# Shift chunks of a modulated input projection moved from TensorE to VectorE, with three edits of banks and loads

## The chip, the cores and the metric

The kernel runs on one core of a Trainium2 chip. The metric is the device time of one execution in microseconds (us). A core has TensorE (PE, matmuls, results in PSUM banks of 128x512 fp32), VectorE (DVE), ScalarE (ACT), GpSimd (POOL) and SyncE (SP, which here only issues loads). Each engine works through its own queue of instructions in order, and waits on semaphores for the others.

## The reference

One layer, in fp32: 512 latent tokens `x` and 256 context tokens `ctx`, width 2048.

```python
mx = silu(c) @ w_mod + b_mod            # and mc from c_ctx, for the context
sh1, sc1, gt1, sh2, sc2, gt2 = split(mx, 6)
hc = rmsnorm(ctx, norm1_g) * (1 + sc1c) + sh1c
hx = rmsnorm(x, norm1_g) * (1 + sc1) + sh1
q, k, v, g, lf, lb, cb, cc, cx = split_proj(hx @ w_in)   # k 512, v 1024 columns; lf, lb 16 each
la_f = log_sigmoid(lf @ w_gf + b_gf) / 16                # la_b likewise
o = gated_linear_attention(q, k, v, la_f, la_b, state_of_context)   # both directions
mix = concat([rmsnorm(o) * gla_g * silu(g), cb * conv3(cc * cx)]) @ w_out
x1 = x + gt1 * mix
h2 = rmsnorm(x1, norm2_g) * (1 + sc2) + sh2
out = rmsnorm(x1 + gt2 * (silu(h2 @ w_ffn_gate) * (h2 @ w_ffn_up)) @ w_ffn_down, final_g)
```

The shift `sh1` (2048 numbers for x, 2048 for the context) is a product of silu(c) with 2048 columns of `w_mod`.

## The kernel before

The inner dimension 2048 is cut into 16 chunks of 128 (`KD`). Tokens stand in six tiles of 128: four of x, two of the context. fp32 operands are split into two parts, hi and lo (`hhi`/`hlo`, for odd chunks side by side in `hhl`, for the context in `chl`), and `mm3` makes a product from three matmuls. Weights arrive as `raw` (128x1024, two K tiles, four buffers), ScalarE casts them to `whi`, and VectorE subtracts for `wlo` (L107).

The stages that matter here:

- K. `scaled_chunk` builds each chunk scaled, but not normalised and not shifted, and K is computed from it. The missing rsqrt (`r6` by token, `rbx` and `rbc` as broadcast rows) is applied to the results.
- First half of V (`wv[0]`), 16 K tiles of 18 matmuls. Alongside, `mod_cols(wsh, ...)` computes four groups of four chunks of the shift on TensorE: 16 blocks of 32 columns into the bank `pm`, a copy, then `pc`, which stands the result up as columns `shs`. From tile 4 on `shift_chunk(i - 4)` makes the chunk final: GpSimd adds hi and lo, VectorE multiplies by the rsqrt row and adds the shift, both split again. `lf_part` computes the low-rank rows (`pl`) from the shifted chunks.
- Second half of V (`wv[1]`), from shifted chunks. Alongside, `shares` adds what the shift contributes to the results that were computed without it: it loads the weights once more and multiplies them by `shs` (`pb`, then `pbc`, `pbk`, `pbx`).
- Context gates and q; then `do_gates`, with `log_gates` (a chain of two Abs, Exp, Ln on ScalarE and two instructions on VectorE, L497) for each token tile; GLA heads, output projection, FFN. During all this `mod_some` computes the other modulation numbers on VectorE: rows of `wm2` multiplied by a broadcast row `cbc` of silu(c) and summed (L405).
- The FFN's down projection works on block combinations: operand pairs `a0h` to `a6l` are loaded from DRAM (`load_ops`), weight parts `ch` as well (`back`), and steps "1", "7", "63", "5" stand in a fixed order. The last group adds by rows (`by_rows`); its last tile is done in two column halves, which share one bank.

Banks come from rings: `bank` has five, `abank` three. The order on each engine is not that of the code: a scheduler sets it when the program is built, from due times of its own, so that a load or a product may stand far from its line.

## Time and profile before

| | |
|---|---|
| median of 3 runs | 2288.15 us (2282.64 to 2289.99) |
| profiled execution | 2291.32 us, span 2289.5 us |
| mean granted clock of TensorE | 0.993 |
| busy: PE, DVE, ACT, POOL | 2241.7, 1658.7, 1002.6, 251.0 us |
| DMA | 433 MB, 189 GB/s over the span |

In the rows of a profile a line starts with the start and the length in us, then come engine, line, operation, outputs<-inputs by the names of the program, and the shape. What stands in brackets is the engine's idle time before and what ended it. `PE acc L94 <- DVE wlo L107: 12.6, 12, 3.2` in a list of waits means 12.6 us in 12 waits, the longest 3.2. Lines of a group give the count, the busy time and the mean in ns.

### The profile page before, as it was taken

The numbers are of one execution on the slowest core, as the hardware profiler recorded it, in microseconds if no ns is written. First come the engines' busy times: TensorE is split into PE (matmuls) and PEld (weight loads), VectorE is DVE, ScalarE is ACT, GpSimd is POOL, SyncE is SP. The second block draws the span as 40 slices with busy tenths as digits, with TensorE's granted clock in tenths as the row PEclk, the third lists the DMA queues.
The fourth block names the chain that finished last, engine by engine and source line by source line (L and its number), as shares of the span: only waits on it lengthen the run. The fifth ranks groups of instructions, "written<-read, shape, count | busy, mean of one in ns | idle before, by whom it ended". The sixth has DMA issues, their size and how long they took to land.

```text
span 2289.5 us, 28001 instructions
## 1 busy us (share of the span) xinstructions
PE 2241.7 (98%) x10258; PEld 1791.7 (78%) x10258; DVE 1658.7 (72%) x2069; ACT 1002.6 (44%) x1354; POOL 251.0 (11%) x396
## 2 busy tenths in 40 slices
PE   8999999999999999999999999999999999999997
PEld 4765666787888887777888888888888878888886
DVE  3566165665768656899788879877987877787885
ACT  3433155333233433665555455445544544433343
POOL 2433100222332000100000000000000000000000
PEclk9999999999999999999999999999999999999999
DMA  9683465566767354624543464345435676756752
GB/s 329 216 279 129 153 221 189 202 220 202 250 228 258 116 198 157 208 69 141 189 156 120 147 210 148 118 159 172 158 131 183 246 291 212 244 193 206 253 174 93
DMA packets 163410, 433.16 MB, mean 189 GB/s; under 512 B 18022, under 2 KB 38790, under 8 KB 163144
## 3 DMA queue, kind: packets, MB, share of 16 engines
q1 hardware_dynamic: 128984, 331.20, 43.3%
q0 software_dynamic: 22416, 78.66, 9.7%
q10 hardware_dynamic: 11872, 21.52, 2.5%
q8 instruction: 81, 1.33, 0.2%
q14 instruction: 57, 0.47, 0.1%
HBM read 380.95 MB, written 50.35 MB: 188 GB/s over the span
## 4 chain that ended last, share of the span: by engine, by line
issue 56%; POOL 2%; PE 1%; DVE 1%; ACT 0%; DMA 0%; POOLq 0%; DVEq 0%; ACTq 0%
POOL opd L1066 2%; PE acc L94 1%; DVE wlo L107 0%; DVE ch L849 0%; DMA out<-g 0%; DVE u L1019 0%; POOL xnd L1022 0%; ACT whi L106 0%; POOL hbig L958 0%; DVE hbig L1020 0%; DVE u L869 0%; POOLq L1066 0%; ACT y L1214 0%; ACT acc L1205 0%; DVE g L1202 0%
## 5 line engine op out<-in xcount | busy, mean ns | idle before, releaser
L106 ACT CAST whi<-ch 128x1024 fp32r<-128x1024 f32 x335 | 352.5, 1053 | 415.4 <-PE acc L94 344.9
L107 DVE TENSOR_TENSOR wlo<-ch,whi 128x1024 fp32r<-128x1024 f32 x335 | 408.2, 1223 | 126.9 <-ACT whi L106 126.0
L106 ACT CAST whi<-raw 128x1024 fp32r<-128x1024 f32 x258 | 270.7, 1050 | 453.6 <-PE acc L94 282.0
L107 DVE TENSOR_TENSOR wlo<-raw,whi 128x1024 fp32r<-128x1024 f32 x258 | 316.6, 1227 | 198.3 <-ACT whi L106 197.7
L94 PE MATMUL acc<-hhl,whi 128*128 128x512 f32 x640 | 200.0, 393 | 0.0
L94 PEld LDWEIGHTS acc<-hhl,whi 128*128 128x128 f32 x640 | 120.8, 189 | 27.6 <-issue 2.5
L1066 POOL DMA_DIRECT2D opd<-ol x80 | 43.3, 541 | 885.8 <-DVE ol L107 885.7
L94 PE MATMUL acc<-hhi,wlo 128*128 128x512 f32 x320 | 134.1, 421 | 5.4 <-DVE wlo L107 4.6
L405 DVE CUSTOM_DVE_ANT_0 wm<-wm,cbc 128x1024 f32<-128x1024 f32 x66 | 80.6, 1224 | 80.9 <-DMA wm<-wm 80.2
L94 PE MATMUL acc<-wlo,a0h 128*128 128x512 f32 x324 | 128.8, 397 | 4.0 <-DVE wlo L107 4.0
L94 PE MATMUL acc<-whi,a6l 128*128 128x512 f32 (+1 forms) x330 | 127.9, 389 | 2.4 <-ACT acc L1205 2.1
L94 PE MATMUL acc<-wlo,a6h 128*128 128x512 f32 (+1 forms) x330 | 128.1, 388 | 1.3 <-DVE wlo L107 1.3
L94 PE MATMUL acc<-whi,a6h 128*128 128x512 f32 (+1 forms) x330 | 127.8, 387 | 0.0
L94 PE MATMUL acc<-whi,a0h 128*128 128x512 f32 x324 | 127.5, 393 | 0.0
L94 PE MATMUL acc<-hlo,whi 128*128 128x512 f32 x320 | 126.9, 397 | 0.2 <-DVE hlo L112 0.2
L94 PE MATMUL acc<-hhl,wlo 128*128 128x512 f32 x320 | 127.0, 397 | 0.0
L94 PE MATMUL acc<-whi,a0l 128*128 128x512 f32 x324 | 126.9, 393 | 0.0
L94 PE MATMUL acc<-whi,a5h 128*128 128x512 f32 x324 | 126.3, 390 | 0.0
L94 PE MATMUL acc<-hhi,whi 128*128 128x512 f32 x320 | 126.2, 394 | 0.0
L94 PE MATMUL acc<-whi,a5l 128*128 128x512 f32 x324 | 126.2, 389 | 0.0
L94 PE MATMUL acc<-wlo,a5h 128*128 128x512 f32 x324 | 126.1, 389 | 0.0
L405 DVE CUSTOM_DVE_ANT_0 raw<-raw,cbc 128x1024 f32<-128x1024 f32 x62 | 75.4, 1223 | 51.4 <-DMA raw<-wm 51.1
(334 smaller groups left out, 4991.8 us busy)
## 6 DMA issues: line engine op xcount, KB each, us to landing
raw<-wu SPq DMA_DIRECT2D x92, 512.0 KB, 4.4
ch<-wu SPq DMA_DIRECT2D x88, 512.0 KB, 3.8
wm<-wm POOLq DMA_DIRECT2D x66, 512.0 KB, 5.3
raw<-wd SPq DMA_DIRECT2D x50, 512.0 KB, 5.3
raw<-wc SPq DMA_DIRECT2D x48, 512.0 KB, 4.7
opd<-oh ACTq DMA_DIRECT2D x80, 256.0 KB, 3.2
opd<-ol POOLq DMA_DIRECT2D x80, 256.0 KB, 3.7
ch<-wd SPq DMA_DIRECT2D x38, 512.0 KB, 4.4
```

What stands on the lines that cost most here:

```text
L94: nc.tensor.matmul(o, l, r, start=start, stop=stop, skip_group_check=True)
L106: nc.scalar.copy(hi, src)
L107: (eng or nc.vector).tensor_tensor(lo, src, hi, op=ALU.subtract)
L405: nc.vector.tensor_tensor_reduce(out=w, in0=w, in1=cbc[:, hf * 1024 : hf * 1024 + 1024], scale=1.0, scalar=0.0, op0=ALU.mult, op1=ALU.add, ...
L1066: nc.gpsimd.dma_start(opd[j][i, 1].rearrange("p k t -> p (k t)"), lo.bitcast(F32))
```

## The change

1. Only the first four chunks of the shift (`NPE`) stay with `mod_cols` on TensorE. For the other twelve `shift_rows` has GpSimd load transposed rows of `w_mod` (`wst`) in halves of 128x1024 and VectorE multiply and sum them: once with `cbc` (for x, 1024 elements) and twice with a part of `ccbc` (for the context, 512 elements each). 20 of the 24 halves stand in the loop of the first half of V, four in the second.
2. The second half of V and the low-rank rows are computed from rows without shift, like K and the first half. `lf_part` adds hi and lo on GpSimd for x and the context; `lf_shift` adds the shift's part later; `shares` gets eight more weight loads and `shared(2)`. The context chunks are never shifted, and the x chunks only in the second half.
3. In `do_gates` the second `pzs` of a pair comes from `abank`. In the first down group the operand loads of S2 and S4 and the weight part of the step "5" change places. In the last group the second column half of the last tile has a bank of its own, and its matmuls are cut in two from the start.

```diff
+NPE = 4
...
     def shift_chunk(i):
-        for n, h, rb, q in ((SEQ, hx[i], rbx, 0), (CTX, hc[i], rbc, 1)):
-            t = big() if q == 0 else hcpool.tile([P, n], F32, tag="sq1", name="ht", bufs=2)
-            nc.gpsimd.tensor_tensor(t, h[0].bitcast(F32), h[1].bitcast(F32), op=ALU.add)
-            nc.vector.tensor_tensor(t, t, rb, op=ALU.mult)
-            sh = shs[:, i, q : q + 1]
-            if q == 0:
-                nc.vector.tensor_scalar(t, t, sh, None, op0=ALU.add)
-                split(h[0], h[1], t)
-                hraw[i] = t
-            else:
-                split_shifted(h[0], h[1], t, sh)
+        h, t = hx[i], big()
+        nc.gpsimd.tensor_tensor(t, h[0].bitcast(F32), h[1].bitcast(F32), op=ALU.add)
+        nc.vector.tensor_tensor(t, t, rbx, op=ALU.mult)
+        split_shifted(h[0], h[1], t, shs[:, i, 0:1])
...
-    def lf_part(pl, g):
-        for j in range(4):
-            mm(pl[32 * j : 32 * j + 32, :], wl3[:, 4 * g + j, :], hraw[4 * g + j], g == 0, g == 3)
-    def lf_finish(pl, a, n):
+    def lf_part(plx, plc, g):
+        tx, tcx = [big() for _ in range(4)], []
+        for c in range(4):
+            i = 4 * g + c
+            if c % 2 == 0:
+                t2 = hcpool.tile([P, 2, CTX], F32, tag="sq0", name="hs", bufs=2)
+            tcx.append(t2[:, c % 2, :])
+            for t, h in ((tx[c], hx[i]), (tcx[c], hc[i])):
+                nc.gpsimd.tensor_tensor(t, h[0].bitcast(F32), h[1].bitcast(F32), op=ALU.add)
+        for pl, t, n in ((plx, tx, SEQ), (plc, tcx, CTX)):
+            for c in range(4):
+                mm(pl[32 * c : 32 * c + 32, :n], wl3[:, 4 * g + c, :], t[c], g == 0, g == 3)
+    def lf_finish(pl, a, n, rb):
         t = hcpool.tile([P, SEQ], F32, tag="lfs", name="lfs", bufs=1)
-        nc.scalar.copy(t[:, :n], pl[:, :n])
+        nc.vector.tensor_tensor(t[:, :n], pl[:, :n], rb, op=ALU.mult)
         ps = bank("ps")
         for q in (0, 64):
             mm(ps[q : q + 32, :n], smt[:, S_QUAD : S_QUAD + 32], t[:, :n], True, True)
         nc.scalar.copy(lfT[:32, a : a + n], ps[:32, :n])
         nc.vector.tensor_copy(lfT[64:96, a : a + n], ps[64:96, :n])
+    def lf_shift():
+        plb, t, b = bank("plb"), modv[:, 16:18], modv[:, 20:22]
+        for k in range(KD):
+            j = 32 * (k % 4)
+            mm(plb[j : j + 32, 0:2], wl3[:, k, :], shs[:, k, 0:2], k < 4, k >= 12)
+        nc.scalar.copy(t, plb[:, 0:2])
+        ps = bank("ps")
+        for q in (0, 64):
+            mm(ps[q : q + 32, 0:2], smt[:, S_QUAD : S_QUAD + 32], t, True, True)
+        for q in (0, 64):
+            nc.vector.tensor_copy(b[q : q + 32], ps[q : q + 32, 0:2])
+            for n, (c0, c1) in enumerate(((0, SEQ), (SEQ, SEQ + CTX))):
+                v = lfT[q : q + 32, c0:c1]
+                nc.vector.tensor_scalar(v, v, b[q : q + 32, n : n + 1], None, op0=ALU.add)
...
+    nc.sync.dma_start(cbc, crow.partition_broadcast(P))
+    nc.scalar.activation(cbc, cbc, AF.Silu)
+    ccbc = [big() for _ in range(4)]
+    for q in range(4):
+        nc.sync.dma_start(ccbc[q], ccrow[q * 512 : q * 512 + 512].partition_broadcast(P))
+        nc.scalar.activation(ccbc[q], ccbc[q], AF.Silu)
+    waste = big()
+    nst = KD - NPE
+    accx = modacc[:, :nst, :]
+    accc = modacc[:, nst : 3 * nst, :].rearrange("p (n q) h -> p n (q h)", q=2)
+    done = [0]
+    def shift_rows(halves, w0):
+        for _ in range(halves):
+            n, hf = divmod(done[0], 2)
+            done[0] += 1
+            w = wpool.tile([P, 1024], F32, tag="raw", name="raw", bufs=4)
+            nc.gpsimd.tensor_copy(w[:, 0:1], w0[0][:, 0, 0:1].bitcast(F32))
+            nc.gpsimd.dma_start(w, wst[n, :, hf * 1024 : hf * 1024 + 1024])
+            for q in (2 * hf, 2 * hf + 1):
+                nc.vector.tensor_tensor_reduce(
+                    out=waste, in0=w[:, q % 2 * 512 : q % 2 * 512 + 512], in1=ccbc[q], scale=1.0, scalar=0.0,
+                    op0=ALU.mult, op1=ALU.add, accum_out=accc[:, n, q : q + 1])
+            nc.vector.tensor_tensor_reduce(
+                out=w, in0=w, in1=cbc[:, hf * 1024 : hf * 1024 + 1024], scale=1.0, scalar=0.0,
+                op0=ALU.mult, op1=ALU.add, accum_out=accx[:, n, hf : hf + 1])
+            if done[0] % 8 == 0:
+                n0 = n - 3
+                for q, acc in enumerate((accx, accc)):
+                    t = modv[:, 4 * q : 4 * q + 4]
+                    nc.vector.tensor_reduce(t, acc[:, n0 : n0 + 4, :], axis=mybir.AxisListType.X, op=ALU.add)
+                    k = NPE + n0
+                    nc.vector.tensor_tensor(shs[:, k : k + 4, q], t, colt[:, C_BMOD + k : C_BMOD + k + 4], op=ALU.add)
     accv = banks6()
-    pl = bank("pl")
     for i in range(KD):
         if i % 2 == 0:
             wvp = load_w(wv[0, i // 2], 2)
         for tt in range(NX + NCT):
             mm3(accv[tt], stat(i, tt), sl(wvp, ALL, i % 2), i == 0, i == KD - 1)
-        if i % 4 == 3:
-            pcs = mod_cols(wsh, i - 3, 4)
-            for c in range(4):
-                nc.vector.tensor_scalar(shs[:, i - 3 + c, 0:2], pcs[:, 2 * c : 2 * c + 2], col(C_BMOD + i - 3 + c),
+        if i == 1:
+            pcs = mod_cols(wsh, 0, NPE)
+            for c in range(NPE):
+                nc.vector.tensor_scalar(shs[:, c, 0:2], pcs[:, 2 * c : 2 * c + 2], col(C_BMOD + c),
                                         None, op0=ALU.add)
-        if i >= 4:
-            shift_chunk(i - 4)
-        if i in (8, 12):
-            lf_part(pl, i // 4 - 2)
+        shift_rows(2 if i % 4 == 1 else 1, wvp)
+        if i in (4, 7, 10, 13):
+            if i == 4:
+                plx, plc = bank("plx"), bank("plc")
+            lf_part(plx, plc, i // 3 - 1)
+    lf_finish(plx, 0, SEQ, rbx)
+    lf_finish(plc, SEQ, CTX, rbc)
...
-    nc.sync.dma_start(cbc, crow.partition_broadcast(P))
-    nc.scalar.activation(cbc, cbc, AF.Silu)
...
-        w = load_raw((wk if i < 8 else wv[0])[i % 8]).rearrange("p (k n) -> p k n", k=2)
+        w = load_raw((wk, wv[0], wv[1])[i // 8][i % 8]).rearrange("p (k n) -> p k n", k=2)
...
+        if i % 8 == 7 and i < 16:
+            shared(i // 8)
...
-        if i < 4:
-            shift_chunk(KD - 4 + i)
-        if i == 1:
-            lf_part(pl, 2)
-        elif i == 5:
-            lf_part(pl, 3)
-            lf_finish(pl, 0, SEQ)
-        if i > 5:
-            for k in ((2 * i - 12, 2 * i - 11) if i < 12 else (i,)):
-                shares(k)
-    for tt in range(NX):
-        for hh in range(2):
-            if tt % 2 == 0:
-                vx[2 + hh][tt // 2] = xpool.tile([P, 2, DV], F32, tag="t", name="vx")
-            nc.scalar.copy(vx[2 + hh][tt // 2][:, tt % 2, :], accv[tt][:, hh * DV : hh * DV + DV])
-    for tt in range(NCT):
-        vc[tt][1] = big()
-        nc.vector.tensor_copy(vc[tt][1], accv[NX + tt])
-    lf_finish(sh_t["pl"], SEQ, CTX)
+        if i < 2:
+            shift_rows(2, wvp)
+        else:
+            for k in (0, 1) if i == 2 else (i - 1,):
+                shift_chunk(k)
+        if i == 3:
+            lf_shift()
+        if i > 3:
+            shares(2 * i - 8)
+            shares(2 * i - 7)
+    from_banks(1)
+    shift_chunk(KD - 1)
+    shared(2)
...
-            pzs = [bank("pzs") for _ in range(2)]
+            pzs = [bank("pzs"), abank("pzs")]
...
+            parts = [(tt, bank8("acc"), 0, NB) for tt in range(NX)]
+            if by_rows and c:
+                h = NB // 2
+                parts[3:] = [(3, parts[3][1], 0, h), (3, bank8("acc"), h, NB)]
...
-            def before_5():
-                if p == 0 and g == 0:
-                    load_ops(g, S2, S4)
-                    back(NPU - 1)
-
-            before = {"5": before_5, "63": before_63}
+            before = {"63": before_63}
+            if p == 0 and g == 0:
+                before["5"] = lambda: back(NPU - 1)
+                before["5", 2] = lambda: load_ops(g, S2)
+                before["5", 3] = lambda: load_ops(g, S4)
...
-        "wsh": w_mod[:, 0:2048].reshape(KD, P, D),
+        "wsh": w_mod[:, : NPE * P].reshape(KD, P, -1),
+        "wst": w_mod[:, NPE * P : 2048].T.reshape(KD - NPE, P, D),
```

Three places show what the built order makes of it. The first is GpSimd in the first half of V; `raw` with a number is one load's buffer, `wst` the new rows. Before, after the casts of the mask:

```order
L273 CAST maskt_83<-cstt_80 128x128 x8
L307 TENSOR_TENSOR big_1299<-hhi_144,hlo_145 128x512
L307 TENSOR_TENSOR big_1328<-hhl_188 128x512
L307 TENSOR_TENSOR big_1363<-hhi_264,hlo_265 128x512
L307 TENSOR_TENSOR ht_1369<-chl_271 128x256
L424 TENSOR_TENSOR hs_2085<-chl_149 128x256
L307 TENSOR_TENSOR ht_1458<-chl_311 128x256
```

After (rows 53 to 60, before these, are eight more adds of the same kind):

```order
L325 TENSOR_TENSOR big_1573<-hhi_615,hlo_616 128x512
L325 TENSOR_TENSOR big_1574<-hhl_656 128x512
L325 TENSOR_TENSOR big_1575<-hhi_732,hlo_733 128x512
L325 TENSOR_TENSOR big_1576<-hhl_773 128x512
L325 TENSOR_TENSOR big_1683<-hhi_849,hlo_850 128x512
L384 COPY raw_1343<-whi_1321 128x1
L384 COPY raw_1391<-whi_1321 128x1
L384 COPY raw_1397<-whi_1321 128x1
L325 TENSOR_TENSOR big_1684<-hhl_890 128x512
L385 DMA raw_1343<-wst 128x1024
```

The adds of thirteen x chunks now stand ahead of the load of the sixth half row (`raw_1343`); before there were three, and no load at all.

The second is VectorE at the same time, around the weight split of K tiles 6 and 7. Before, with `wlo_1342` for these tiles:

```order
L371 TENSOR_TENSOR big_1069<-big_1069,big_1096 128x512
L371 TENSOR_TENSOR big_1071<-big_1071,big_1096 128x512
L371 TENSOR_TENSOR big_1073<-big_1073,big_1096 128x512
L107 TENSOR_TENSOR wlo_1342<-raw_1339,whi_1341 128x1024
L107 TENSOR_TENSOR wlo_1466<-raw_1463,whi_1465 128x1024
L308 TENSOR_TENSOR big_1299<-big_1299,big_1096 128x512
L308 TENSOR_TENSOR big_1328<-big_1328,big_1096 128x512
L308 TENSOR_TENSOR big_1363<-big_1363,big_1096 128x512
L355 TENSOR_SCALAR silsh_85<-pc_1266,colt_75 128x2 x4
```

After, with `wlo_1410` for these tiles:

```order
L410 TENSOR_SCALAR silsh_85<-pc_1244,colt_75 128x2 x4
L109 TENSOR_TENSOR wlo_1322<-raw_1319,whi_1321 128x1024
L387 ISA big_1138,modacc_76<-raw_1343,big_1128 128x512
L387 ISA modacc_76 128x1
L387 ISA big_1138,modacc_76<-raw_1343,big_1129 128x512
L387 ISA modacc_76 128x1
L109 TENSOR_TENSOR wlo_1410<-raw_1407,whi_1409 128x1024
L390 ISA raw_1343,modacc_76<-raw_1343,cbc_79 128x1024
```

Two reduces of the half row `raw_1343` stand ahead of the split that TensorE needs, where before the split followed products of K (L371) and stood ahead of all but the first chunks of the shift.

The third is the seam of the two halves of V. On TensorE, after:

```order
L96 MATMUL acc6_1144<-whi_1707,chl_1013 128x512
L96 MATMUL ps_1761<-lfs_1759,smt_74 32x512 x2
L96 MATMUL acc6_1793<-whi_1801,hlo_145 128x512
L96 MATMUL acc6_1793<-wlo_1802,hhi_144 128x512
L96 MATMUL acc6_1793<-whi_1801,hhi_144 128x512
L96 MATMUL acc6_1794<-whi_1801,hlo_145 128x512
L96 MATMUL ps_1768<-lfs_1766,smt_74 32x256 x2
L96 MATMUL acc6_1794<-wlo_1802,hhi_144 128x512
```

and on VectorE, after:

```order
L390 ISA raw_1823,modacc_76<-raw_1823,cbc_79 128x1024
L390 ISA modacc_76 128x1
L387 ISA big_1138,modacc_76<-raw_1829,big_1128 128x512
L387 ISA modacc_76 128x1
L427 TENSOR_SCALAR big_1785<-acc6_1143,rs_r_1088 128x512
L427 TENSOR_SCALAR big_1787<-acc6_1144,rs_r_1088 128x512
L333 TENSOR_TENSOR lfs_1766<-plc_1350,big_1097 128x256
L338 COPY lfT_82<-ps_1761 32x512
```

Before, the last shift group (`pm`) and the start of the second half stood here on TensorE:

```order
L94 MATMUL pl_1130<-big_1679,big_1120 32x512
L94 MATMUL pm_1776<-big_1813,silsh_85 32x512
L94 MATMUL pm_1776<-big_1816,silsh_85 32x512
L94 MATMUL acc6_1869<-whi_1877,hlo_145 128x512
L94 MATMUL acc6_1869<-wlo_1878,hhi_144 128x512
L94 MATMUL acc6_1869<-whi_1877,hhi_144 128x512
```

The matmul `ps` on `lfs_1766` now stands ahead of all but four matmuls of the second half, and `lfs_1766` stands on VectorE behind the half row `raw_1823` and a part of the next.

104 lines of the change are left out of this document (51 added, 53 removed).

## The prediction

> **What bounds the kernel now.** I read the page's busy times first, then a table of stages for the part that the change rewrites, then the list of waits of TensorE, and last the timeline around each wait.
>
> ```profile
> PE 2241.7 (98%) x10258; PEld 1791.7 (78%) x10258; DVE 1658.7 (72%) x2069; ACT 1002.6 (44%) x1354; POOL 251.0 (11%) x396
> ```
> ```profile
> 110.77:128.90 18.13, 18.13 (x86) 14.76 (x85) 9.29 (x22) 7.21 (x8) 0.00 (x0) 1.00 0.93 318
> 128.90:152.30 23.40, 23.40 (x114) 15.46 (x113) 17.26 (x23) 6.15 (x10) 12.37 (x11) 1.00 0.74 246
> 152.30:178.59 26.29, 25.72 (x122) 15.40 (x121) 17.23 (x26) 6.81 (x11) 9.76 (x8) 1.00 0.62 212
> ...
> 217.30:300.01 82.71, 82.64 (x401) 55.40 (x402) 25.13 (x42) 15.58 (x26) 12.11 (x16) 1.00 0.41 140
> ```
> ```profile
> PE acc L94 <- DVE wlo L107: 12.6, 12, 3.2
> PE pzs L94 <- DVE hbig L497: 2.5, 1, 2.5
> PE acc L94 <- ACT acc L1205: 2.1, 1, 2.1
> ```
>
> The first row says that TensorE is occupied 98% of the span, so a wait that is taken away, or matmuls that are taken away, shorten the kernel about one for one, and every new wait of TensorE lengthens it. The stages (start and end, length, then busy time and instructions of each engine) are from the two halves of V. The first half begins at 110.77 and ends at 204.88, and the first matmul of q follows the second at 300.01; the stage left out, 178.59 to 204.88, is like the one before it. TensorE is full in all of them, VectorE is at 17.2 of 26.3 us, GpSimd at 9.8. The three waits are those that the smaller edits touch; they are among the longest of TensorE.
>
> **TensorE's own work.** A stage of four K tiles holds 72 matmuls of 128x512.
>
> ```profile
> 1841.80 0.39 PE L94 MATMUL acc<-wlo,a0h 128*128 128x512 f32 x1
> ...
> 1842.93 0.61 PE L94 MATMUL acc<-whi,a0l 128*128 128x512 f32 x2
> ```
>
> Five starts lie 1.13 us apart here, so 0.227 each and 16.3 for a stage. In the stage from 152.30 on 26.29 - 16.3 = 10 us are left: one group of shift columns (pm, its pc and a short wait for a load) and one pl block of 1.1, so a group costs 8.9. Three of four groups go: -26.7. The group that stays cost 23.4 - 16.3 = 7.1; it is now cut by matmuls into twelve pieces. A lone block of four 32-column matmuls takes as long as a full one, 1.07, so 12.8 and 0.95 for pc: +6.7. Eight more weight loads go through pb:
>
> ```profile
> L94 PE MATMUL pb<-raw,silsh 128*32 128x512 f32 x64 | 11.9, 601 | 0.0
> ```
>
> Sixteen loads cost 11.9, so eight cost +6.0; the added pbc and pbx are one more pair (+1.9) and the sixteen two-column matmuls with their two ps +2.5 (an estimate from 0.24 us each where pc has two columns, four side by side). The low-rank blocks only change place. Sum: -10 us, if nothing waits. With bounds of 0.7 and 1.07 for a lone block the sum lies between -14 and -10; the interleaving speaks for the upper price.
>
> **What VectorE and GpSimd get.** Twenty of 24 half rows of the twelve chunks run inside the first half of V: each is one 128x1024 reduce and two of 128x512. At the same time GpSimd adds hi and lo of all sixteen chunks there (sixteen 128x512, sixteen 128x256), because the low rank now reads the unshifted rows early, and it issues the 20 row loads, each behind a small copy. Whether these two engines run side by side decides the case. Rows from the first half of V before, GpSimd then VectorE:
>
> ```profile
> 154.28 1.61 POOL L307 TENSOR_TENSOR big<-hhl 128x512 f32<-128x512 f32 x1 [5.53 <-PE pm L94]
> 155.86 1.27 POOL L307 TENSOR_TENSOR big<-hhi,hlo 128x512 f32<-128x512 f32 x1
> 157.08 1.72 POOL L307 TENSOR_TENSOR big<-hhl 128x512 f32<-128x512 f32 x1
> 158.76 1.71 POOL L307 TENSOR_TENSOR big<-hhi,hlo 128x512 f32<-128x512 f32 x1
> ...
> 155.93 3.42 DVE L308 TENSOR_TENSOR big<-big 128x512 f32<-128x512 f32 x2 [1.18 <-POOL big L307]
> 159.27 1.49 DVE L311 TENSOR_SCALAR big<-big,silsh 128x512 f32<-128x512 f32 x1
> ...
> 186.96 1.28 DVE L308 TENSOR_TENSOR big<-big 128x512 f32<-128x512 f32 x2
> ```
> ```profile
> L308 DVE TENSOR_TENSOR big<-big 128x512 f32<-128x512 f32 x16 | 18.4, 1182 | 3.5 <-POOL big L307 3.5
> L311 DVE TENSOR_SCALAR big<-big,silsh 128x512 f32<-128x512 f32 x16 | 12.5, 782 | 0.0
> ```
>
> A product of 128x512 takes 0.64 in the pair at 186.96. In the pair at 155.93 it takes 1.71, and the row of its line has a mean of 1182 ns. Its start follows the end of GpSimd's first add, it ends 0.6 after the end of the second, and GpSimd's third add (1.72 where the second took 1.27) ends 1.2 after the product: they take turns. The add of a scalar at 159.27 ends just after GpSimd's fourth. The reduce does it too:
>
> ```profile
> 651.64 2.37 POOL L392 COPY wm<-whi 128x1 f32<-128x1 f32 x2 [4.62 <-ACT whi L106]
> 651.46 1.23 DVE L405 CUSTOM_DVE_ANT_0 wm<-wm,cbc 128x1024 f32<-128x1024 f32 x1 [4.11 <-DMA wm<-wm]
> 652.73 1.23 DVE L405 CUSTOM_DVE_ANT_0 raw<-raw,cbc 128x1024 f32<-128x1024 f32 x1
> ```
>
> Two copies of one column took 2.37 us, as long as the two reduces beside them. So I count VectorE's two-input instructions and GpSimd's in one queue. The Trainium skill, page "SBUF — State Buffer", section "Who interferes with whom", has this as a rule: a VectorE instruction with two SBUF inputs and a GpSimd instruction that reads SBUF exclude each other for their whole length. The trace agrees (1.71 for 0.64); by the opposite rule of two free engines the sum would be that of the first rival.
>
> Prices, from the rows of the same instructions elsewhere, with the load's time to landing:
>
> ```profile
> 348.16 1.23 DVE L405 CUSTOM_DVE_ANT_0 raw<-raw,cbc 128x1024 f32<-128x1024 f32 x1 [3.07 <-DMA raw<-wm]
> 349.45 1.23 DVE L405 CUSTOM_DVE_ANT_0 raw<-raw,cbc 128x1024 f32<-128x1024 f32 x1
> 146.44 0.74 POOL L424 TENSOR_TENSOR hs<-chl 128x256 f32<-128x256 f32 x1
> wm<-wm POOLq DMA_DIRECT2D x66, 512.0 KB, 5.3
> ```
>
> The reduces start 1.29 apart. A 128x512 reduce is nowhere in the trace: 0.64 (a product) below, 1.23 above; I take 0.8, half the long one with its own read of the sum. A half row is then 1.29 + 2 x 0.8 = 2.9 us. Adds are 1.27 and 0.74, a split of a weight (L107) 1.22.
>
> **Four places where TensorE waits.** I laid the built orders beside each other from 107 us on, with these prices.
>
> *Start of V.* ScalarE's rows:
>
> ```profile
> 107.47 1.05 ACT L106 CAST whi<-raw 128x1024 fp32r<-128x1024 f32 x1
> 108.43 0.58 ACT L278 COPY big<-acc 128x512 f32<-128x512 f32 x1
> 110.46 1.28 ACT L147 ACT_TABLE_LOAD   x1
> L375 ACT ACTIVATE cbc<-cbc 128x2048 f32<-128x2048 f32 x1 | 1.9, 1916 | 1.5 <-DMA cbc<-crow 1.5
> ```
>
> The split of V's first weight follows at 107.47 now. In the new order the Silu of cbc (1.92), two copies, the table load (1.28) and the root stand ahead of it: 108.43 + 0.6 + 1.9 + 0.6 + 1.3 + 0.2 + 1.0 = 114.1. TensorE is ready for V at 110.8 (the first stage's start) and waits 3.2. A wait of that length has a second price, seen in the row of 1846.76 below: fourteen matmuls take 6.14 us instead of 3.2, so 2.9 more. Together 6.1.
>
> *K tile 6.* TensorE reaches it at about 159.5 (114.1 + 6 x 4.1 + 2.9 + the 12.8 of pm and some 5 for pc and pl). GpSimd has thirteen adds in a row ahead of the load of raw_1343. They can start when the buffers of pm's operands come free, about 135, and take 13 x 1.27 plus some six turns of 0.8 = 21 to 22. Copies, one more add and the issue (0.54) put the load at 159.3; it lands 4.4 to 5.3 later, and VectorE must do two of its reduces (with two adds between, 3 us) ahead of wlo_1410 (1.2): 168. A wait of 8.4, and 2.9 after it: 11.3. Without turns it would be 1 to 2.5.
>
> *From tile 6 to the end of the first half.* A pair of tiles brings 2.5 half rows (7.2), a weight split (1.2), copies (0.5) and adds (12.7 us in five pairs, 2.5): 11.4 on the common queue against 8.2 + 1.2 for TensorE. Five pairs lose 10 us. At the end the matmul ps on lfs_1766 stands ahead of most of the second half, and lfs_1766 behind two and a third half rows, 6.7 us, of which TensorE's lead covers some 2. So 15 us in two long waits and a short one, with 2.9 after each long one: 21. Without turns a pair costs 8.9, the rate is met, and 5.5 to 8.4 at the end remain.
>
> *Second half.* The two-column matmuls need the sums of all rows. After the seam VectorE has four half rows (11.6), a weight split (1.2) and five products with the adds they wait for (3.5 + 6.3): 22.6, against 16.3 + 2.9 for TensorE: a wait of 3.4 to 3.8. The copies of its result 2, one late weight 2, the copy before pbc 0.8: 9, and 2.9: 11.7. Without turns 1.
>
> Sum for the two halves: 6.1 + 11.3 + 21 + 11.7 - 10 = +40; without turns 3.2 + 2 + 7 + 1 - 10 = +3, and with 2.9 after the longer waits +12.
>
> **The other three edits.** The gates:
>
> ```profile
> 355.72 1.23 DVE L405 CUSTOM_DVE_ANT_0 raw<-raw,cbc 128x1024 f32<-128x1024 f32 x1 [1.34 <-DMA raw<-wm]
> 356.87 1.29 DVE L497 SCALAR_TENSOR_TENSOR hbig<-pzs,lg 128x512 f32<-128x512 f32 x2
> 357.62 1.85 PE L94 MATMUL pzs<-gatet,lfT 33*128 33x512 f32 x2 [2.50 <-DVE hbig L497]
> ```
>
> The third pair of pzs waits for the L497 of the first, which stood behind two reduces waiting for loads. In the new order it stands ahead of them: 2.5 and some 2.8 after it go. But the second pzs now takes a bank of the ring of q and g, and the unit that gets this bank next has to wait for the whole chain of ScalarE (two 0.6, two table loads of 1.28, 1.06 and 1.15 per tile, and a cast: 7.2) which is longer than a round of TensorE (6.8). I take -2, with -5 and +2 as ends. Operand loads:
>
> ```profile
> 1835.90 2.36 SPq L795 DMA_DIRECT2D ch<-wd  x4
> 1841.94 1.22 DVE L824 TENSOR_TENSOR ch<-ch 128x1024 f32<-128x1024 f32 x1 [3.46 <-DMA ch<-wd]
> 1846.76 0.80 PE L94 MATMUL acc<-wlo,a0h 128*128 128x512 f32 x1 [3.21 <-DVE wlo L107]
> 1852.90 0.41 PE L94 MATMUL acc<-wlo,a0h 128*128 128x512 f32 x1
> ```
>
> VectorE's L824 waits for b0, issued behind sixteen operand loads, and the weight split of the next step stands behind it. In the new order b0 and b1 are issued right behind the four loads before the operands, ahead of all sixteen: b0 lands before 1830, and the 3.2 and the 2.9 go: -6, with -3 as the other end if an operand pair is late instead. The last tile:
>
> ```profile
> 2276.20 0.58 PE L94 MATMUL acc<-whi,a6l 128*128 128x256 f32 x1 [2.05 <-ACT acc L1205]
> ...
> 2280.14 0.43 DVE L1202 TENSOR_TENSOR g<-acc,hbig 128x256 f32<-128x256 f32 x1 [2.28 <-PE acc L94]
> ```
>
> The right half gets its own bank: 2.05 and 18 short matmuls at 0.21 instead of 0.12 go, 0.2 is added for cutting kh = 0. TensorE so ends 3.7 earlier; but VectorE, which begins the last half at 2280.14, has tile 2 to finish until about 2278, so the gain lies between 1.8 and 3.7; I take -2.5.
>
> Sum: +40 - 2 - 6 - 2.5 = +29.5 on the profiled 2291.32, so 2320.8. That execution is 3.2 above the median of the runs (2288.15), which gives 2317.6; the prices of the long waits are rounded up, so I say 2316.
>
> **Rivals.**
> 1. The two engines do not hinder each other: +12 and -10.5, so +1.5 and 2290, no change. For it speaks only that no 128x512 reduce is in the trace; against it all the rows above.
> 2. The other side: VectorE keeps up altogether. Its sums are hidden, TensorE's -10 and -10.5 arrive: 2268. It decides at one point: wlo_1410 has to be ready by 159.5, so GpSimd must have issued raw_1343 by 150, nine us earlier than I get. If the buffers come free earlier than the pm operands suggest, the thirteen adds are over in time.
> 3. Worse: row loads from GpSimd's queue land in 7 us rather than 5.3, while four slots serve rows and weights in turn; nine loads on the path add 15: 2332.
>
> **Chances.** The forecast 0.67, rival 1 0.15, rival 2 0.09, rival 3 0.09. About 0.3% (6.9 us) is what a measurement of this kernel can tell from no change. Rival 2 and a little of 1 give faster, 0.10; most of rival 1 and the lowest tail of the forecast give no change, 0.13; the rest is slower, 0.77. The range leaves out rival 2 below and the end of 3 above: 2287 to 2334. The forecast's own range is 2300 to 2328.
>
> **What would show it.** Right: TensorE waits of about 3 us near 111, 8 near 160, 5 near 190 and 8 near 225, each released by VectorE's wlo or lfs (the first by ScalarE's whi); GpSimd adds of 1.7 and more and reduces stretched beyond 1.23; q starting near 340 instead of 300; no waits at the places of 357.6, 1846.8 and 2276.2. Wrong: reduces of 1.23 throughout beside busy GpSimd, or raw_1343 loaded before 150.

## The result, and the profile after

The changed kernel takes 2310.51 us (median of 4 runs, 2309.30 to 2313.07) where the kernel before takes 2289.07 (4 runs beside it): a ratio of 1.0103, 95% interval 1.0088 to 1.0117. By the medians it is 21 us slower. The forecast was 2316, slower, with a range of 2287 to 2334. The profiled execution of after is 2310.51 us, its span 2308.4, 18.9 more than before.

The busy times of after, first row of the page:

```profile
PE 2236.5 (97%) x10228; PEld 1790.7 (78%) x10228; DVE 1707.7 (74%) x2184; ACT 999.0 (43%) x1338; POOL 288.4 (12%) x444
```

TensorE is busy 5 us less, VectorE 49 and GpSimd 37 more, and the kernel is longer: this row does not tell why. The table of stages does. Its columns are start and end, length, busy time of TensorE, of its weight loads, VectorE, ScalarE and GpSimd, then the granted clock of TensorE. First the V part of before, from its sums of squares (`pss`) to the first context gate (`pzs`), then the same of after:

```profile
109.50:305.00 195.50, 193.47 (x921) 124.73 (x919) 98.04 (x155) 51.27 (x83) 51.59 (x48) 1.00 0.56 189
```
```profile
111.10:332.20 221.10, 194.57 (x863) 125.18 (x861) 140.24 (x258) 45.73 (x67) 82.52 (x94) 0.92 0.53 182
```

V is 25.6 us longer. The stage of before also holds ten matmuls of q, about 2.3 us, which now stand behind its end; like for like V is some 28 us longer. TensorE waits 26.4 us in it (1.8 before), and its clock is 0.92 on average where it was 1.00. TensorE is busy as long as before only because it runs slower: a table by single microseconds has the clock near half in five stretches, and its busy time there, times what the clock lacks of 1, comes to about 12 us. So 25.6 = 24.6 of new waits + 12 of clock - 11 of work, of which 2.3 are the matmuls of q that only moved. The longest waits of TensorE in V and the gates, from the timeline:

```profile
115.33 0.51 PE L96 MATMUL acc<-whi,hlo 128*128 128x512 f32 x1 [2.82 <-ACT whi L108]
...
169.44 0.50 PE L96 MATMUL acc<-wlo,hhi 128*128 128x512 f32 x1 [1.86 <-DVE wlo L109]
...
196.05 0.50 PE L96 MATMUL acc<-wlo,hhi 128*128 128x512 f32 x1 [2.17 <-DVE wlo L109]
...
236.45 0.64 PE L96 MATMUL ps<-lfs,smt 128*32 128x256 f32 x2 [9.75 <-DVE lfs L333]
...
256.78 0.28 PE L96 MATMUL plb<-silsh,big 128*32 128x2 f32 x8 [2.42 <-DVE silsh L399]
...
390.21 0.80 PE L96 MATMUL acc<-hhi,wlo 128*128 128x512 f32 x1 [6.23 <-DVE hbig L553]
```

The largest stands at the seam, as forecast, on the product `ps` of `lfs`. The wait at tile 6 (169.44) is 1.86 instead of 8.4. The other stages together give back 6.7: +1.6 ahead of V, gates (to `pk`, with those matmuls of q) +0.6, heads -3.3, the rest -8.0 up to TensorE's last matmul and +2.4 behind it.

What VectorE waits for between 111 and 260, and how long its reduces take (groups: count, busy time, mean ns):

```profile
DVE big L387 <- DMA raw<-wst: 20.4, 7, 9.9
DVE silsh L410 <- PE pc L96: 12.3, 1, 12.3
```
```profile
L387 DVE CUSTOM_DVE_ANT_0 big<-raw,big 128x512 f32<-128x512 f32 x48 | 39.3, 818 | 22.9 <-DMA raw<-wst 20.4 <-ACT big L371 1.9
L390 DVE CUSTOM_DVE_ANT_0 raw<-raw,cbc 128x1024 f32<-128x1024 f32 x24 | 35.1, 1462 | 0.6
```

Two things show. The reduces are stretched (1462 ns where one alone takes 1.23 us). And VectorE, on which TensorE waits, itself stands idle for 33 us, for rows that have not landed and for `pc`. An engine that is late and idle is not short of time; something ahead of it comes late.

### The profile page after: what moved, and what is told of

The parts are those of the page before. It is cut to its first block, busy times and chain, and to the rows that moved or that the text cites. A ratio compares the mean times of both kernels' runs of the same rounds, so it can differ in the third digit from the quotient of the medians.

```text
span 2308.4 us, 28023 instructions
## 1 busy us (share of the span) xinstructions
PE 2236.5 (97%) x10228; PEld 1790.7 (78%) x10228; DVE 1707.7 (74%) x2184; ACT 999.0 (43%) x1338; POOL 288.4 (12%) x444
## 4 chain that ended last, share of the span: by engine, by line
issue 29%; PE 25%; DVE 3%; POOL 1%; DMA 1%; ACT 0%; POOLq 0%; DVEq 0%; ACTq 0%
PE acc L96 24%; DVE wlo L109 1%; POOL opd L1126 1%; DMA raw<-wu 1%; PE pt L1112 1%; DVE ch L905 1%; PE pt L1030 0%; DVE u L925 0%; ACT whi L108 0%; ACT y L1273 0%; DVE hbig L1080 0%; DMA out<-g 0%; DVE u L1079 0%; DVE s L832 0%; DVE a6l L109 0%
## 5 line engine op out<-in xcount | busy, mean ns | idle before, releaser
L461 DVE CUSTOM_DVE_ANT_0 wm<-wm,cbc 128x1024 f32<-128x1024 f32 x66 | 80.7, 1224 | 79.4 <-DMA wm<-wm 78.7
```

The costliest lines, as they stand in the source:

```text
L461: nc.vector.tensor_tensor_reduce(out=w, in0=w, in1=cbc[:, hf * 1024 : hf * 1024 + 1024], scale=1.0, scalar=0.0, op0=ALU.mult, op1=ALU.add, ...
```

## The experiments

All are compared with the kernel before on the same chip. The edits are against the changed kernel unless another is named.

**The three small edits alone**, on the kernel before; V is that of before.

```diff
-            pzs = [bank("pzs") for _ in range(2)]
+            pzs = [bank("pzs"), abank("pzs")]
...
+            if p == 0 and g == 0:
+                before["5"] = lambda: back(NPU - 1)
+                before["5", 2] = lambda: load_ops(g, S2)
+                before["5", 3] = lambda: load_ops(g, S4)
...
+                parts[3:] = [(3, parts[3][1], 0, h), (3, bank8("acc"), h, NB)]
```

> The kernel before with the three small edits alone (second pzs of a pair from the ring of three banks, order of the operand loads, own bank for the last half tile); V as before. In the changed kernel the stretch from the context gates to the first head came out 0.5 us shorter against before, the heads 5 us shorter, the first down group 6.2, the end 1.0. Theory A: all of that belongs to the three edits, the 5 us of the heads to the bank of pzs too: -0.5 - 5 - 6.2 - 1.0, so 12 to 13 us below before, near 2277. Rival B: the 5 us of the heads come from the new V (tiles and buffers fall otherwise there): -7.5, near 2282, and TensorE waits for po behind the sum of the first heads as long as before (four waits of 1.1 to 2.6 us). In both the wait at 1846.8 (3.2 us) is gone.

**The same without the gates' bank**, again on the kernel before.

```diff
-            pzs = [bank("pzs"), abank("pzs")]
+            pzs = [bank("pzs") for _ in range(2)]
```

> The kernel before with the order of the operand loads and the bank of the last half tile, but not the gates' bank. Theory A (the gates' bank costs: the first wait of acc behind the second chain, 6.2 us, for two waits of 2.5 and 1.6): 2.5 us below e1_three_edits, 2281 to 2282, pk begins 103.7 after the first context gate instead of 106.0. Rival B (the gates come out even): 2284 as e1_three_edits.

With the bank 2283.98 us (ratio 0.9985, 0.9974 to 0.9996), without it 2281.49 (0.9970, 0.9957 to 0.9982). So by the medians the bank costs 2.5 us. The two intervals overlap a little, so the sign is likely rather than certain; with the bank the first B's 2282 is the closer guess, and without it the time is the second A's 2281 to 2282. The stretch from the first context gate to `pk` is 106.0 us with it, 102.8 without (103.7 before), in one execution each. The row shows how, in the kernel with the bank:

```profile
364.62 0.79 PE L94 MATMUL acc<-hhi,wlo 128*128 128x512 f32 x1 [6.23 <-DVE hbig L497]
```

The old wait for the third pair of `pzs` shrank from 2.50 to 1.50 and a new one of 6.23 came behind it: the next unit of q gets the bank that the gates hold until their chain on ScalarE is through. The heads tell nothing of the bank: 386.6 us before, 384.1 with it, 388.4 without, all within what they vary by anyway (next section).

**The gates' bank back in the changed kernel** (the same two lines).

> The changed kernel with both pzs from the ring of five banks, as before the change. Theory A: the bank of three is what makes acc wait 6.2 us behind the second chain of the gates; that wait goes, the old one of about 2.5 us for the third pair of pzs comes back with a slower stretch of 2.9 us behind it, and the heads lose their 5 us again: slower by 0 to 6 us, 2311 to 2317. Rival B: the heads' gain is V's doing: the 6.2 us go, 2.5 + 2.9 come: 2309 to 2311.

2309.93 us, ratio 1.0101 (1.0080 to 1.0121), against 1.0103: the two cannot be told apart, as B expected. In the profiled execution (2300.89, the shortest of five) the wait of 6.23 is gone, and one of 3.28 at a weight split has come.

**V without GpSimd's adds.** The low rank takes hi and lo by two matmuls.

```diff
     def lf_part(plx, plc, g):
-        tx, tcx = [big() for _ in range(4)], []
...
-                nc.gpsimd.tensor_tensor(t, h[0].bitcast(F32), h[1].bitcast(F32), op=ALU.add)
-        for pl, t, n in ((plx, tx, SEQ), (plc, tcx, CTX)):
-            for c in range(4):
-                mm(pl[32 * c : 32 * c + 32, :n], wl3[:, 4 * g + c, :], t[c], g == 0, g == 3)
+        for pl, src, n in ((plx, hx, SEQ), (plc, hc, CTX)):
+            for p in range(2):
+                for c in range(4):
+                    i = 4 * g + c
+                    mm(pl[32 * c : 32 * c + 32, :n], wl3[:, i, :], src[i][p].bitcast(F32),
+                       g == 0 and p == 0, g == 3 and p == 1)
```

> The changed kernel with the low-rank rows made from hi and lo by two matmuls each instead of one on their sum: the 32 adds of GpSimd in the first half of V (33 us when undisturbed) go, TensorE gets 32 more matmuls of 32 columns (4 blocks of 1.07 and 4 of about 0.55 us: +6.5). Theory A (GpSimd's adds hold up VectorE, by their turns and by standing ahead of the row loads): the load of raw_1343 is issued before 145, the reduces of 128x1024 take 1.23 each, VectorE's lateness at the seam is gone, and with it the waits of 1.9, 1.7, 2.2 and 9.8 us and two or three slower stretches of 2.9: -22 + 6.5, so about 2295. Rival B (VectorE has too much work by itself: 24 half rows of 2.7 us): the 9.8 us stay in the main; 2308 to 2317. Rival C (row loads land late): reduces wait for raw as before, 20 us in the first half; 2308 to 2317.

2308.64 us, ratio 1.0097 (1.0077 to 1.0116). Theory A has failed: taking away GpSimd's 32 adds does not by itself bring the time back. The second matmuls cost TensorE some 3 us in V (its busy time less what the slow clock cost is 185.7 us there and 182.5 in the changed kernel), so taking away the adds was worth some 5 us, not 22. The time is that of B and C, and the trace speaks for C in part: the reduces of 128x1024 come down to 1294 ns, and VectorE still waits for rows, which were issued late rather than slow to land (5.7 us at the median, 5.3 before the edit). At the seam the adds of `shift_chunk`, which stayed, still stretch a reduce of 0.69 to 5.03. The wait for rows:

```profile
DVE big L382 <- DMA raw<-wst: 17.3, 8, 4.0
```

**V without half of VectorE's reduces.** The 48 reduces of 128x512 go; the sums for the context's shift are left out, so the result for the context is another one.

```diff
+    nc.vector.memset(accc, 0.0)
...
-            for q in (2 * hf, 2 * hf + 1):
-                nc.vector.tensor_tensor_reduce(
-                    out=waste, in0=w[:, q % 2 * 512 : q % 2 * 512 + 512], in1=ccbc[q], scale=1.0, scalar=0.0,
-                    op0=ALU.mult, op1=ALU.add, accum_out=accc[:, n, q : q + 1])
```

> The changed kernel without the 48 reduces of 128x512 (the context's shift of twelve chunks stays zero plus its bias; the result for the context is another one). VectorE loses 48 x 0.82 = 39 us in V; GpSimd and TensorE keep all they do. Theory A (turns with GpSimd, row loads behind its adds): raw_1343 is still issued near 160, but a half row then costs 1.3 to 2.3 instead of 2.7 to 4, so VectorE is level again at the seam: the wait of 9.8 us and the later of the shorter ones go, with two slower stretches: about 2292 to 2296. Rival B (VectorE's own work is too long): the same gain or a little more, 2288 to 2296, and every wait for wlo gone. Rival C (loads land late): the waits at 169 and 236 stay, 2305 to 2311.

2310.60 us, ratio 1.0098 (1.0078 to 1.0119). So 39 us less work on the engine that TensorE waits for bring nothing that the time shows; A and B have both failed. C has the time, but not the whole reason: the loads land in 6.0 us at the median (5.3 in the changed kernel), and the wait near 169 is down to 0.77. VectorE waits 10 us longer for rows and is shut out once for 9 (below):

```profile
DVE raw L387 <- DMA raw<-wst: 30.3, 11, 6.3
```

The wait at the seam even grew to 16.46. VectorE's row there, then the first and last of nine GpSimd adds beside it:

```profile
219.56 10.48 DVE L387 CUSTOM_DVE_ANT_0 raw<-raw,cbc 128x1024 f32<-128x1024 f32 x1 [4.39 <-DMA raw<-wst]
```
```profile
217.94 1.27 POOL L307 TENSOR_TENSOR big<-hhi,hlo 128x512 f32<-128x512 f32 x1
...
227.69 1.25 POOL L307 TENSOR_TENSOR big<-hhi,hlo 128x512 f32<-128x512 f32 x1
```

A reduce of 1.23 lasts 10.48 us. It begins while the second of the adds runs, and ends 1.1 after the last of them: it did not get a turn in the whole row.

**The same with `shift_chunk`'s sums on VectorE.**

```diff
-        nc.gpsimd.tensor_tensor(t, h[0].bitcast(F32), h[1].bitcast(F32), op=ALU.add)
+        nc.vector.tensor_tensor(t, h[0].bitcast(F32), h[1].bitcast(F32), op=ALU.add)
```

> As e4_no_ctx_sums (no 128x512 reduces, so another result for the context), and the sum of hi and lo in shift_chunk on VectorE instead of GpSimd (16 x 0.7 = 11 us more for VectorE, GpSimd idle at the seam). In e4_no_ctx_sums one reduce lasted from 219.56 to 230.04, and nine adds of GpSimd in a row ended at 228.94. Theory A (a VectorE instruction that arrives while GpSimd runs back to back waits until the run is over): that reduce takes 1.23, the wait of ps for lfs shrinks from 16.5 to about 7: 2299 to 2303. Rival B (the reduce waited for its row, whose load was late): it stays near 10 us long: 2309 to 2314.

2300.10 us, ratio 1.0056 (1.0040 to 1.0073), inside what A expected: VectorE got 11 us more work, and the kernel became 10 us shorter. The reduce at the same place:

```profile
219.58 1.23 DVE L387 CUSTOM_DVE_ANT_0 raw<-raw,cbc 128x1024 f32<-128x1024 f32 x1 [4.20 <-DMA raw<-wst]
```

The wait at the seam is 9.64 now rather than 7, since VectorE still waits for rows ahead of it (4.20 here).

**Rows not tied to a cast.** Each row load stands behind a copy of one column out of its tile's `whi`, so it cannot start before ScalarE has cast that weight.

```diff
-            nc.gpsimd.tensor_copy(w[:, 0:1], w0[0][:, 0, 0:1].bitcast(F32))
             nc.gpsimd.dma_start(w, wst[n, :, hf * 1024 : hf * 1024 + 1024])
```

> The changed kernel without the one-column copies alone; GpSimd's adds stay. The sixth row load then stands ahead of the eight-add run of GpSimd instead of behind thirteen adds. Theory A (turns: VectorE and GpSimd together have too much to do, wherever the loads stand): 2304 to 2311, reduces stretched as in the changed kernel. Rival B (late row loads are the cause, whether by the tie or by the adds ahead of them): as much gained as e9_no_anchor over e3_no_adds, 2298 to 2303, no wait for rows over 3 us.

2308.81 us, ratio 1.0101 (1.0073 to 1.0129): no gain. Rows are early now, no wait of VectorE for one is left in the list, but it meets GpSimd's adds all the time:

```profile
L386 DVE CUSTOM_DVE_ANT_0 big<-raw,big 128x512 f32<-128x512 f32 x48 | 47.4, 988 | 2.3 <-ACT big L371 1.5
L389 DVE CUSTOM_DVE_ANT_0 raw<-raw,cbc 128x1024 f32<-128x1024 f32 x24 | 40.2, 1675 | 0.7
```
```profile
164.50 7.03 DVE L386 CUSTOM_DVE_ANT_0 big<-raw,big 128x512 f32<-128x512 f32 x1
...
172.73 0.79 PE L96 MATMUL acc<-wlo,hhi 128*128 128x512 f32 x1 [10.31 <-DVE wlo L109]
```

The two groups take 87.6 us; undisturbed they take 62.4 (below). Theory A is right here: 25 us go to the turns.

**Both: no adds and no ties** (the edit above on the kernel without adds).

> As e3_no_adds (low rank from hi and lo, no adds of GpSimd in the first half), and without the one-column copy ahead of each row load, which ties a load to the cast of its tile's weights: a row load now starts as soon as one of the four raw buffers is free. In e3_no_adds VectorE was idle 17.3 us for rows and 12.9 for pc between 111 and 260. Theory A (rows come late because of the tie, and VectorE is late for that): the wait for rows falls below 6, the seam's waits (6.9, 4.8, 3.6) go in the main: 10 to 16 below e3_no_adds, 2293 to 2299. Rival B (VectorE's own work and its wait for pc set the seam): 2303 to 2309. Rival C (rows take the buffers that weights need): new waits for whi and wlo, 2309 or more.

2299.04 us, ratio 1.0046 (1.0031 to 1.0061), at the upper end of A. Each of the two edits alone brought 2 us or less, both together 11. What each of them left standing made VectorE late in its own way, and either was enough. What is left is at the seam: VectorE comes to it late by a reduce of 5.87 (0.69 alone) beside four adds of `shift_chunk` and two more of 2.28 and 2.16 (1.23 alone) in turns with such adds, and it idled 13.6 us for `pc` earlier:

```profile
229.02 0.64 PE L96 MATMUL ps<-lfs,smt 128*32 128x256 f32 x2 [9.12 <-DVE lfs L328]
```

**The order at the seam.**

```diff
     lf_finish(plx, 0, SEQ, rbx)
-    lf_finish(plc, SEQ, CTX, rbc)
...
-        if i == 3:
+        if i == 4:
+            lf_finish(plc, SEQ, CTX, rbc)
+        if i == 9:
             lf_shift()
```

> The changed kernel with two things later in the second half of V: the finish of the context's low-rank row (lfs of plc, then ps) after its fifth K tile instead of ahead of the half, and lf_shift after its tenth tile instead of its fourth. Nothing is taken away. Theory A (the loss at the seam is one of order: a matmul that nobody needs yet stands in TensorE's queue ahead of the second half, and its operand on VectorE stands behind the last half rows): the waits of 9.75, 2.42 and 1.33 us and the slower stretch behind them go, 4 to 5 us come back at the second weight split of the half, which stands behind the same half rows: 8 to 12 below the changed kernel, 2298 to 2302. Rival B (VectorE is late by the sum of its work): the same 13 us appear at the weight splits: 2307 to 2312.

2306.85 us, ratio 1.0089 (1.0070 to 1.0109): some 4 us, close to what B expected. The wait moved to the next things that stand behind the same rows, a bank that VectorE has to empty and the second weight split of the half:

```profile
234.60 0.79 PE L96 MATMUL acc<-whi,chl 128*128 128x512 f32 x1 [5.02 <-DVE big L426]
...
255.78 0.51 PE L96 MATMUL acc<-wlo,hhi 128*128 128x512 f32 x1 [4.96 <-DVE wlo L109]
```

**The same, the Silu rows behind V's first weight, and the gates' bank back.**

```diff
-    nc.sync.dma_start(cbc, crow.partition_broadcast(P))
-    nc.scalar.activation(cbc, cbc, AF.Silu)
...
-        nc.scalar.activation(ccbc[q], ccbc[q], AF.Silu)
...
+        if i == 0:
+            for t, src in ((cbc, crow), *((ccbc[q], ccrow[q * 512 : q * 512 + 512]) for q in range(4))):
+                nc.sync.dma_start(t, src.partition_broadcast(P))
+                nc.scalar.activation(t, t, AF.Silu)
```

> As e5_seam, and the Silu of the two broadcast rows behind the load and split of V's first weight instead of ahead, and both pzs from the ring of five banks. Theory A: the start's wait of 2.8 us (and up to 2.9 for the slower stretch behind it) goes, the gates give 2.5; 4 to 8 us below e5_seam, 2291 to 2297. Rival B: the Silu, once later, is late for the first half rows, which then push the seam: no gain over e5_seam but the 2.5.

2302.76 us, ratio 1.0063 (1.0043 to 1.0082), 4 below the one before: the least of the gain that A expected, at a time past A's 2291 to 2297, and most of it can be the gates' bank, as B had it. The wait of 2.82 at the start is gone, and this one has come at tile 6:

```profile
162.47 0.79 PE L96 MATMUL acc<-wlo,hhi 128*128 128x512 f32 x1 [8.09 <-DVE wlo L109]
```
```profile
158.88 0.72 DVE L382 CUSTOM_DVE_ANT_0 big<-raw,big 128x512 f32<-128x512 f32 x1 [14.39 <-DMA raw<-wst]
```

That is about the wait of 8.4 that the forecast had there. In the changed kernel TensorE comes to the same place late and finds most of it over.

**All of it**: no adds, `shift_chunk`'s sums on VectorE, no ties, the seam, the Silu rows, the gates' bank back, and the four columns out of `pc` written by ScalarE. Of these only the last has not stood above:

```diff
-                nc.vector.tensor_scalar(shs[:, c, 0:2], pcs[:, 2 * c : 2 * c + 2], col(C_BMOD + c),
-                                        None, op0=ALU.add)
+                nc.scalar.activation(shs[:, c, 0:2], pcs[:, 2 * c : 2 * c + 2], AF.Identity, bias=col(C_BMOD + c))
```

> e6_seam_start_gate with four more things: low rank from hi and lo without GpSimd's adds (+6.5 of TensorE), shift_chunk's sum on VectorE, the four columns out of pc written by ScalarE instead of VectorE, and row loads not tied to a cast. GpSimd then has no arithmetic at all in V. Theory A (all of V's loss is queue order and the shared turn, none is bandwidth): TensorE's waits in V fall from 27 us to under 8, V is as long as before (195.5 from the first pss to the first context gate, 215.7 in e6_seam_start_gate), and with the operand loads and the tail the whole is 2278 to 2286. Rival B (the four raw buffers, which weights and rows share, limit the rows whatever the order): V keeps 10 us or more over before, 2291 to 2300.

2280.00 us, ratio 0.9956 (0.9941 to 0.9970): inside what A expected, the lowest median of all, 10 us below before by its ratio and 30 below the changed one by the medians. Against the version above, four things are added (no adds, the sums on VectorE, no ties, the columns by ScalarE); what each is worth by itself was not tried in it, but for the tie (next). And the operand loads and the last half tile alone, on the kernel before, had come to 2281.49 (0.9957 to 0.9982): the intervals overlap, so the whole time does not show that moving the shift is worth anything by itself, even in this order. The V part and VectorE's reduces in it:

```profile
109.20:293.60 184.40, 180.77 (x929) 120.33 (x928) 131.17 (x270) 46.24 (x70) 12.22 (x23) 1.00 0.63 215
```
```profile
L375 DVE CUSTOM_DVE_ANT_0 big<-raw,big 128x512 f32<-128x512 f32 x48 | 33.0, 688 | 2.0 <-DMA raw<-wst 1.2
L378 DVE CUSTOM_DVE_ANT_0 raw<-raw,cbc 128x1024 f32<-128x1024 f32 x24 | 29.4, 1224 | 0.7
```

V is 11 us shorter than before (9 without the matmuls of q), TensorE waits 3.6 us in it, its clock is 1.00, and VectorE does all of the twelve chunks' reduces with nothing in its way.

**All of it, with the ties back** (the one-column copy).

> e10_all with the one-column copies back, which tie each row load to the cast of its tile's weights. GpSimd has nothing else to do in V. Theory A (the tie is a cost of its own: rows come late, VectorE idles for them and is late at the seam): the gain that e9_no_anchor had over e3_no_adds, about 10 us, is lost again, 2288 to 2294, VectorE waits over 10 us for rows between 111 and 260. Rival B (the tie costs only where GpSimd's adds, VectorE's wait for pc or the order at the seam use up the slack): 2279 to 2284, V at most 4 us longer than 184.3.

2292.23 us, ratio 1.0018 (1.0008 to 1.0029). As theory A expected, the tie alone costs 12 us. The reduces last 688 and 1224 ns as without it, and VectorE waits:

```profile
DVE big L376 <- DMA raw<-wst: 20.6, 8, 5.7
```
```profile
110.30:311.90 201.60, 185.58 (x927) 122.71 (x925) 131.22 (x270) 46.32 (x70) 26.47 (x47) 0.96 0.58 199
```

V is 17 us longer than with everything; the heads were 9 shorter in this trace.

The heads change from trace to trace without a change of their code (next section), so the length of V, from `pss` to the first `pzs`, is the steadier measure. In the profiled executions it is 221.1 us in the changed kernel, 219.9 without the adds, 217.1 without half of the reduces and 209.1 with the sums on VectorE as well, 217.0 without the ties, 205.2 with neither adds nor ties, 219.5 with the order at the seam, 215.7 with the start as well, 184.4 with everything and 201.6 with the ties back. A single edit is worth 1 to 4 us there, no adds and no ties together 16, and everything 37.

## Why the prediction was right, and where its reason fell short

The side came out, and so did the places of the four main waits of V and what releases them; the time is 5.5 us below the forecast. Part of that closeness is luck: the steps add up to 29.5 us where the profiled executions lie 19.2 apart, and 4.8 us had been taken off on the way from the sum to 2316. The range of 2287 to 2334 would have held for no change, too. Step by step:

- *TensorE's own work, -10.* It is about -9 in the changed kernel by the account above, without the matmuls of q. In the version with everything V has 180.8 us of TensorE at full clock, 10.4 below before without those matmuls, though it makes the low rank twice. The sum is right by terms that are off both ways: by the busy times three shift groups with their `pc` were worth 22 us (29.7 for four), not 26.7, and the eight more loads of `pb` cost 0.9 (12.8 in all against 11.9), not 6.0. The twelve pieces of the group that stays took 13.2, close to the 12.8 forecast.
- *Waits of V, some 36, and 14 for the clock behind them.* Measured 24.6 more than before, and 12. The start had 2.82 of 3.2. Tile 6 had 1.86 of 8.4: the row load of `raw_1343` was issued at 161.4 (forecast 159.3) and `wlo_1410` was done at 169.4 (168). These times are close, but by luck: the thirteen adds began at 139.4, not at 135, and turns cost them less than 1 us, not 5, because VectorE stood idle for `pc` from 142 to 154; GpSimd waited 3.4 us for buffers instead. What failed is TensorE's side: it was to be there at 159.5 and came near 167.6, 8 later. It started 1.2 later, lost 4.8 to the slow clock instead of 2.9, and spent 2 (at full clock) on the row broadcasts `pr`, which the sum did not have; for the other 3 no single term was found. The version with the Silu rows moved shows the wait of 8.09. From tile 6 to the end of the half some 15 were forecast, and 1.7, 2.2, 0.7 and the 9.75 at the seam came (and 0.8 beside the 1.7), 15 in all. In the second half 2.4, 1.3, 0.6 and 0.8 came for 9.
- *VectorE's two-input instructions and GpSimd's in one queue.* True: the reduces last 988 and 1675 ns beside the adds, 688 and 1224 without GpSimd's arithmetic. The Trainium skill, page "SBUF — State Buffer", section "Who interferes with whom", has the two exclude each other for the length of an instruction. The trace agrees that they exclude each other, but not with that length. The turns were priced at one instruction each; the runs showed one reduce shut out for eight adds in a row (10.48 us).
- *This as what decides the case.* Half of the truth. Neither taking the adds away nor halving the reduces changed the time measurably. The step that failed is the one that took the prices of two engines and added them to a rate (11.4 on the common queue against 9.4 for TensorE). A rate would have improved with either edit. What sets the time is a chain in queue order, which the forecast followed only at tile 6 and, for its last part, at the seam: a load tied to a cast, its landing, its reduces, and only then the weight split or the `lfs` that TensorE needs. At the seam the rows read so: the cast of the second half's first weight begins at 222.39, the row tied to it is in use at 228.39, its reduces and the next go on to 234.6 (1.65, 2.16 and 1.74 beside GpSimd's adds), `lfs` at 235.89.

```profile
222.39 1.05 ACT L108 CAST whi<-raw 128x1024 fp32r<-128x1024 f32 x1 [8.34 <-DMA raw<-wv]
...
228.39 0.69 DVE L387 CUSTOM_DVE_ANT_0 big<-raw,big 128x512 f32<-128x512 f32 x1 [1.57 <-DMA raw<-wst]
...
229.12 1.65 DVE L387 CUSTOM_DVE_ANT_0 big<-raw,big 128x512 f32<-128x512 f32 x1
...
230.81 2.16 DVE L390 CUSTOM_DVE_ANT_0 raw<-raw,cbc 128x1024 f32<-128x1024 f32 x1
...
235.89 0.41 DVE L333 TENSOR_TENSOR lfs<-plc,big 128x256 f32<-128x256 f32 x1
```

Removing adds leaves the tie, removing the tie leaves the adds. Both together gave 11, and the order at the seam, `pc`, the start, the gates' bank and the last adds 19 more.

- *Gates, -2 (-5 to +2).* +2.5 by the medians on the kernel before, with intervals that overlap: likely past the upper end, by the mechanism that was named for that end (the next unit waits for the bank behind ScalarE's chain). In the changed kernel no difference can be told.
- *Operand loads, -6.* -6.2 between two points of the FFN in the two traces, and the wait at 1846.76 is gone.
- *Last tile, -2.5.* -1.0. On the kernel before, this and the loads together gave 8.0 by the medians, 8.5 were forecast. In the changed kernel TensorE's end lies 3.4 closer; 2.4 are given back, since VectorE takes up the last half 0.7 behind TensorE's end and then waits 1.29 for ScalarE's square.
- *Heads.* They were 3.3 shorter in the profiled execution, which no step had. Their length goes from 379.7 to 393.2 over the fourteen profiles of this study, in which their code is the same. Why was not found.

Of the rivals, the first (engines side by side) and the third (loads of 7 us; the median was 5.3) did not come. The second, VectorE keeps up, is what the version with everything reaches: there the sums are hidden, and its V is 11 us shorter than before. Its time of 2268 was not reached (2280.00).

## What to carry to other kernels

When an engine that others wait for is itself idle, look for what its next instruction waits for before counting its work: here 39 us of its work could go without a gain that the time shows. Two causes of the same lateness hide each other, so an edit that brings nothing alone is not refuted until it has been tried together with the next one. And a load that is tied to another engine's progress to keep it from coming too early needs a check of how late it may be: here the tie alone was worth 12 us.

## What the hardware showed that was not expected

In these traces a VectorE instruction with two SBUF inputs was shut out at times for as long as GpSimd had adds in a row: 10.48 us for one of 1.23 (eight adds, counted from the one in progress), 7.03 for one of 0.69 (five), 5.87 for one of 0.69 (four). Elsewhere the two went in turns, as at 229.12 in the changed kernel, where a reduce of 0.69 took 1.65 between the first add and the second. What decides between the two was not found.

The price of a wait of TensorE changes from trace to trace. The same wait at the same matmul of the FFN, and the 3 us behind it with the clock in the last column but two, first before, then after:

```profile
1003.25 0.50 PE L94 MATMUL acc<-whi,a1l 128*128 128x512 f32 x1 [2.18 <-DVE a1l L107]
```
```profile
1003.25:1006.25 3.00, 3.00 (x13) 2.50 (x14) 3.00 (x5) 1.22 (x2) 0.00 (x0) 1.00 0.00 0
```
```profile
1027.89 0.79 PE L96 MATMUL acc<-whi,a1l 128*128 128x512 f32 x1 [2.18 <-DVE a1l L109]
```
```profile
1027.89:1030.89 3.00, 3.00 (x7) 2.42 (x8) 3.00 (x5) 1.22 (x2) 0.00 (x0) 0.51 0.00 0
```

Before the change the 2.18 us cost nothing more; after it the clock was half behind the same wait. In the traces of before, after, the version without ties and the one with everything, every wait from 2.4 us on was followed by a slow stretch, but for those in the first 13 us of the kernel (two in each trace, 2.61 to 4.16 us, with a clock of 1.00 behind them); of those between 1.5 and 2.2 some were. The Trainium skill, page "TensorE: Matmul & The Clock Gate", section "What's actually happening", puts the slow clock behind an idle window of about 3.4 us that runs free of the kernel. A free window fits a price that changes; the length does not fit, since waits of 1.5 to 2.2 us were enough in some cases, and from 2.4 us on in all behind the first 13 us.
